# A decoder layer on one core: both branch products of a token half side by side, and the second FFN weight prepared in half-column sets

## The chip, the cores and the metric

The kernel runs on one core of one Trainium2 chip. A core has four compute engines that matter here, each with its own instruction stream that it works through strictly in order: TensorE (PE) multiplies matrices, VectorE (DVE) works element by element on two inputs, ScalarE (ACT) applies functions or copies, GpSimd (POOL) does element-wise work too. SyncE (SP) issues the DMAs, also in order. Engines wait for each other through semaphores. The metric is the device time of the program in microseconds; less is better.

## The reference, cut to what matters

One layer on 1024 tokens of 1024 channels, in float32. Two attention branches A and B (the first 800 us, hardly touched by the change) give `o_a` and `o_b`; then:

```python
merged = (jax.nn.sigmoid(g_a) * (o_a @ w_branch_a[l])
          + jax.nn.sigmoid(g_b) * (o_b @ w_branch_b[l]))
x = _layer_norm(ALPHA * x + merged @ w_out[l], ln1_g[l], ln1_b[l])
gate, up = jnp.split(x @ w_ffn_in[l], 2, axis=-1)
ffn = (jax.nn.silu(gate) * up) @ w_ffn_out[l]
x = _layer_norm(ALPHA * x + ffn, ln2_g[l], ln2_b[l])
```

`w_branch_*` is 512 x 1024, `w_ffn_in` 1024 x 5632, `w_ffn_out` 2816 x 1024.

## The kernel before, in words

**Three products for one.** Every float32 operand of a large product is split into a high part (ACT copies it into a rounded type, `whi`, `w[:, 0]`) and a low part (the rest, by a subtraction on POOL for weights or DVE for activations). `mm3` (lines 95 to 101) then issues three matmuls of 128 x 512 for each term: L99 takes high by high, L100 weight low, L101 activation low. A weight tile is therefore of use only when DMA, ACT and POOL have all been at it.

**Branch stage.** `branch(br, ...)` does all 1024 tokens of branch 0 first: it loads and splits `odr`, and for each of eight column blocks c multiplies both token halves, multiplies by the gate tile `g` (read from `gdr`, four buffers, L549) and writes the result to `mdr` in DRAM. Then the same for branch 1, with `emit_b` reading `mdr` back (`m`, two buffers), adding it and splitting the sum into `MH`, `ML` (L649 to L651). `load_w` loads one tile of `wbr` for two c and both halves (L92 on ACT, L93 on POOL for 1024 columns at once), and a tile of `wout` after every second c.

**Output product and transition.** The `wout` product with its layer norm fills `Y`, then transposes (`turn`, L699 to L701) make the activations of the FFN in the forms that a Strassen-Winograd scheme wants. `c11` of the first `AHEAD` = 2 column blocks (24 matmuls each) is done between the turns.

**FFN1.** A loop over 22 column blocks c. Each has seven products of 12 matmuls: `c11` is two of them, then come s2, s3, s1, s4, a22. Four weight sums r1 to r4 are made on DVE (L818 to L821, tag `ss`, four buffers), each is split by ACT (L770) and POOL (L771), and the products are added up from PSUM (L787 for `c11`, L838 five products in six additions); L846 and L847 are the two gating products m1 and m0. At every odd c one pair j is complete: `wb` (one buffer) gets four quarter blocks of `w_ffn_out` (two loads of 512 KB), which are stored raw three times (L859), combined by four DVE instructions of 128x512 (L860 to L863) and stored four times (L865) into `abd`; the two `h` tiles are treated likewise, stored at L868, combined in place at L869 to L872, stored at L874. So each pair has fourteen 256 KB stores.

**FFN2.** Seven passes p over eleven pairs j; `prepare` loads a 512 KB tile `abd[p][j]` holding both operands and splits it (L898 ACT, L899 DVE, L900 POOL). `closing` adds up the passes and ends in the layer norm; in the last pass the last `LASTC` = 6 tiles are multiplied token tile by token tile so that the norms overlap with products.

**What sets the order.** PE's order is the order in which the code is written (`manual_schedule`). The order on ACT, DVE, POOL and SP is made by a scheduler from priorities and buffer rings when the program is built; at run time every engine keeps to that list.

Of the kernel before, what the change touches and what calls it, by code (L numbers as in the profile page):

```python
# [20 lines left out]
KT = 8  # L21
# [17 lines left out]
AHEAD, LASTC, HURRY = 2, 6, 100  # L39
# [10 lines left out]
def trunk_kernel(ctx: ExitStack, tc: tile.TileContext, xT, xn, wt, wbr, wout, wfi, wfo,  # L50
# [17 lines left out]
    def f(ap):  # L68
        return ap.bitcast(F32)
# [34 lines left out]
    XH = [xm.tile([128, KT, 512], F32R, name=f"xh{h}", tag="x", bufs=4) for h in range(2)]  # L104
    XL = [xm.tile([128, KT, 512], F32R, name=f"xl{h}", tag="x", bufs=4) for h in range(2)]
# [17 lines left out]
    mdr = dram.tile([8, 128, L], F32, name="mdr")  # L123
# [407 lines left out]

    def branch(br, oh, ol, emit):
        for k in range(4):
            raw = bp.tile([128, L], F32, name="oraw", tag="oraw", bufs=2)
            sp.dma_start(raw, odr[br][k])
            act.activation(oh[k], raw, AF.Copy)
            dve.tensor_tensor(ol[k], raw, f(oh[k]), op=OP.subtract)
        for c in range(8):
            if c % 2 == 0:
                wh, wl = load_w(wbr[br, c // 2])  # L540
            b0 = (c % 2) * 512
            for h in range(2):
                s = slice(h * 512, h * 512 + 512)
                g = bp.tile([128, 512], F32, name="g", tag="g", bufs=4)
                sp.dma_start(g, gdr[br][c, :, s])
                ps = ps_b()
                mm3(ps, [(wh[:, b0 + k * 128:b0 + k * 128 + 128], wl[:, b0 + k * 128:b0 + k * 128 + 128],
                          oh[k][:, s], ol[k][:, s]) for k in range(4)])
                dve.scalar_tensor_tensor(g, g, 1.0, ps, op0=OP.add, op1=OP.mult)  # L549
                emit(c, h, g)  # L550
            if c % 2:
                k = br * 4 + c // 2
                load_w(wout[k * 128:k * 128 + 128], WOH[k], WOL[k])

# [84 lines left out]
    OA = [xm.tile([128, 4, L], F32R, name=f"oa{x}", tag="x", bufs=4) for x in range(2)]  # L639
    MH, ML = [], []  # L640
    for h in range(2):
        MH.append(xm.tile([128, KT, 512], F32R, name=f"mh{h}", tag="x", bufs=4))
        ML.append(xm.tile([128, KT, 512], F32R, name=f"ml{h}", tag="x", bufs=4))
    OB = [[bp.tile([128, L], F32R, name=f"ob{x}{k}") for k in range(4)] for x in range(2)]

    def emit_b(c, h, g):
        m = bp.tile([128, 512], F32, name="m", tag="m", bufs=2)
        sp.dma_start(m, mdr[c, :, h * 512:h * 512 + 512])
        dve.tensor_tensor(g, g, m, op=OP.add)  # L649
        act.activation(MH[h][:, c], g, AF.Copy, scale=0.5)  # L650
        dve.scalar_tensor_tensor(ML[h][:, c], g, 0.5, f(MH[h][:, c]), op0=OP.mult, op1=OP.subtract)  # L651

    branch(0, [OA[0][:, k] for k in range(4)], [OA[1][:, k] for k in range(4)],
           lambda c, h, g: sp.dma_start(mdr[c, :, h * 512:h * 512 + 512], g))
    branch(1, OB[0], OB[1], emit_b)
# [6 lines left out]
    fin, _fin = open_pool("fin")  # L662
    Y = [fin.tile([128, D], F32, name=f"y{t}") for t in range(NB)]
    for t in range(NB):
        sp.dma_start(Y[t], xn[t * 128:t * 128 + 128])
# [67 lines left out]
    for t in range(NB):  # L733
        half, c0 = divmod(t * 128, 512)
# [73 lines left out]
    ring[0:0] = [(ffl, f"wt{k}", 1) for k in range(4)]  # L808
    for c in range(FC):
# [7 lines left out]
        r1, r2, r3, r4 = (ffl.tile([128, 512], F32, name="ss", tag="ss", bufs=4) for _ in range(4))  # L817
# [30 lines left out]
        if c % 2 == 0:  # L848
            even = h
            continue  # L850


        j = c // 2
        wb = ffl.tile([128, 2, 1024], F32, name="wb", tag="wb", bufs=1)
        for x in range(2):
            sp.dma_start(wb[:, x], wfo[(c - 1 + x) * 128:(c + x) * 128])
        b11, b12, b21, b22 = wb[:, 0, 0:512], wb[:, 0, 512:1024], wb[:, 1, 0:512], wb[:, 1, 512:1024]
        for p, b in ((1, b11), (2, b21), (3, b22)):
            sp.dma_start(abd[p][j][:, 1], b)  # L859
# [4 lines left out]
        for p, b in ((5, b11), (7, b12), (6, b22), (4, b21)):  # L864
            sp.dma_start(abd[p][j][:, 1], b)  # L865
# [3 lines left out]
        dve.tensor_tensor(a22, a21, a22, op=OP.add)  # L869
        dve.tensor_tensor(a21, a11, a21, op=OP.subtract)  # L870
        dve.tensor_tensor(a11, a22, a11, op=OP.subtract)
        dve.tensor_tensor(a12, a12, a11, op=OP.subtract)  # L872
        for p, a in ((5, a22), (7, a21), (6, a11), (3, a12)):
            sp.dma_start(abd[p][j][:, 0], a)  # L874
# [12 lines left out]
    def prepare(p, j):  # L887
        k = len(fring)
        fring.append(None)
        if k % 2 == 0:  # L890
# [4 lines left out]
        raw = wp.tile([128, 1024], F32, name="wraw", tag="wraw", bufs=2) if k < 7 or k % 3 == 0 else \  # L895
            fe.tile([128, 1024], F32, name="fraw", tag="fraw", bufs=4)
# [21 lines left out]
    def closing(p, t, ps):  # L918
# [5 lines left out]
        elif p == 2:  # L924
            scaled(y[:, ha], ps)
            plus(y[:, ha], u)
            dve.bn_stats(bs[:, 0, :], y[:, ha])
        elif p == 6:
            plus(u, ps)
        elif p == 5:  # L930
            v = fy.tile([128, 512], F32, name="v", tag="v", bufs=2)
            plus(v, ps, u)
# [99 lines left out]
```

## Time and profile before

| | us |
|---|---|
| median of three runs (1681.66 to 1690.01) | 1688.73 |
| the profiled execution | 1686.29 |
| its span | 1684.4 |
| PE busy in it | 1606.5 (95%) |
| DVE, ACT, POOL busy | 1160.9, 771.7, 671.3 |

The profile is one execution. Its page gives busy times of the engines; further views of the same trace list what an engine waited for, the busy time by stretch of the span, groups of instructions by line, the chain of waits, and single instructions in order of time. The stages in this execution: branch products 800 to 911 us, output product 911 to 998, turns and `c11` ahead 998 to 1031, FFN1 1031 to 1457, FFN2 1457 to the end.

### The profile page before, as it was taken

Reading aid. Unit: us, or ns where it says so; the run is one execution under the profiler, and the core shown is the slowest. Engines: PE = TensorE matmul, PEld = TensorE weight load, DVE = VectorE, ACT = ScalarE, POOL = GpSimd, SP = SyncE. Lnnn points to the kernel's source line nnn. Section 1 sums busy time; section 2 is a strip of 40 time slices with the busy share of each in tenths; the row PEclk is TensorE's granted clock in tenths of the full one; section 3 lists DMA queues with packets and bytes.
Section 4 is the critical chain, followed back from the end, with each engine's and each line's share of the span. In section 5 each row is a group of like instructions: output and inputs, shape, how many; then the busy total and the mean of one; then the engine's idle time right before and its main releaser. Section 6 shows DMA issues by size and latency. Waiting matters only on the chain. (4 is left out here: it accounts for less than half of the span.)

```text
span 1684.4 us, 22398 instructions
## 1 busy us (share of the span) xinstructions
PE 1606.5 (95%) x7722; PEld 1312.0 (78%) x7722; DVE 1160.9 (69%) x2016; ACT 771.7 (46%) x1368; POOL 671.3 (40%) x646
## 2 busy tenths in 40 slices
PE   7898999998999999999989998999899999999997
PEld 5776887776888888888767876887778888878885
DVE  6889999979645454544466668868786665557577
ACT  6777878884444444544322024222233323254341
POOL 1122333332333333333432036444455444377673
PEclk9999999999999999999999998999999999999998
DMA  5112212121222222223886115677643332497652
GB/s 176 47 40 65 60 45 59 57 70 43 57 68 61 70 57 74 59 63 124 272 257 242 77 51 175 233 247 257 234 160 120 106 107 93 143 342 272 190 165 93
DMA packets 83817, 216.18 MB, mean 128 GB/s; under 512 B 10164, under 2 KB 14260, under 8 KB 83704
## 3 DMA queue, kind: packets, MB, share of 16 engines
q1 hardware_dynamic: 83704, 214.75, 39.0%
q8 instruction: 61, 1.00, 0.2%
q14 instruction: 52, 0.43, 0.1%
HBM read 139.93 MB, written 65.87 MB: 122 GB/s over the span
## 5 line engine op out<-in xcount | busy, mean ns | idle before, releaser
L99 PE MATMUL mm<-xh,whi 128*128 128x512 f32 (+1 forms) x720 | 296.4, 412 | 15.5 <-ACT whi L146 6.4
L101 PE MATMUL mm<-xl,whi 128*128 128x512 f32 (+1 forms) x720 | 281.9, 392 | 1.2 <-DVE xl L156 1.2
L100 PE MATMUL mm<-xh,wlo 128*128 128x512 f32 (+1 forms) x720 | 281.4, 391 | 0.5 <-DVE wlo L147 0.5
L478 POOL TENSOR_SCALAR p<-p,st 128x512 f32<-128x512 f32 (+1 forms) x192 | 113.3, 598 | 321.3 <-DVE st L475 268.6
L93 POOL TENSOR_TENSOR wlo<-wraw,whi 128x1024 fp32r<-128x1024 f32 x51 | 123.1, 2414 | 192.3 <-ACT whi L92 171.0
L771 POOL TENSOR_TENSOR w<-ss,w 128x512 fp32r<-128x512 f32 x88 | 130.4, 1496 | 165.6 <-ACT w L770 158.2
L101 PEld LDWEIGHTS mm<-xl,whi 128*128 128x128 f32 x720 | 136.1, 189 | 32.2 <-DVE xl L156 2.4
L99 PEld LDWEIGHTS mm<-xh,whi 128*128 128x128 f32 x720 | 136.9, 190 | 29.6 <-issue 6.4
L100 PEld LDWEIGHTS mm<-xh,wlo 128*128 128x128 f32 x720 | 137.3, 191 | 13.0 <-DVE wlo L147 1.0
L503 DVE TENSOR_TENSOR pl<-T,ph 128x512 fp32r<-128x512 f32 (+1 forms) x160 | 100.7, 634 | 36.6 <-ACT ph L502 34.7
L99 PE MATMUL acc<-fs 128*128 128x512 f32 x308 | 120.4, 391 | 2.8 <-ACT fs L898 2.8
L101 PE MATMUL acc<-fs 128*128 128x512 f32 x308 | 120.5, 391 | 0.6 <-POOL fs L900 0.6
L100 PE MATMUL acc<-fs 128*128 128x512 f32 x308 | 120.4, 391 | 0.2 <-DVE fs L899 0.2
L502 ACT ACTIVATE ph<-T 128x512 fp32r<-128x512 f32 (+1 forms) x160 | 87.3, 552 | 38.8 <-PE T L501 34.5
L309 ACT ACTIVATE junk<-sm,nt 128x1024 bf16<-128x1024 f32 (+2 forms) x93 | 96.8, 1040 | 14.6 <-DVE nt L317 12.8
L501 PE MATMUL T<-identf,p 128*128 128x128 f32 x576 | 90.5, 273 | 4.8 <-POOL p L478 2.5
L501 PEld LDWEIGHTS T<-identf,p 128*128 128x128 f32 x576 | 71.2, 140 | 26.8 <-POOL p L478 4.4
L900 POOL TENSOR_TENSOR fs<-fraw,fs 128x512 fp32r<-128x512 f32 x47 | 80.7, 1730 | 27.8 <-ACT fs L898 27.8
L511 PE MATMUL O<-pl,V 128*128 128x256 f32 x320 | 82.8, 282 | 1.8 <-DVE pl L503 1.8
L510 PE MATMUL O<-ph,V 128*128 128x256 f32 x320 | 83.6, 283 | 0.0
L899 DVE TENSOR_TENSOR fs<-fraw,fs 128x512 fp32r<-128x512 f32 x47 | 54.4, 1169 | 39.8 <-ACT fs L898 39.8
L771 POOL TENSOR_TENSOR w<-wraw,w 128x512 fp32r<-128x512 f32 x44 | 64.8, 1485 | 35.7 <-ACT w L770 26.9
(278 smaller groups left out, 4107.5 us busy)
## 6 DMA issues: line engine op xcount, KB each, us to landing
fraw<-abd SPq DMA_DIRECT2D x47, 512.0 KB
wraw<-in_wt_dram SPq DMA_DIRECT2D x45, 512.0 KB
abd<-wb SPq DMA_DIRECT2D x77, 256.0 KB
abd<-h SPq DMA_DIRECT2D x77, 256.0 KB
wraw<-abd SPq DMA_DIRECT2D x30, 512.0 KB
wraw<-in_wfi_dram SPq DMA_DIRECT2D x24, 512.0 KB
wup<-in_wfi_dram SPq DMA_DIRECT2D x22, 512.0 KB
wb<-in_wfo_dram SPq DMA_DIRECT2D x22, 512.0 KB
```

What stands on the lines that cost most here:

```text
L93: pool.tensor_tensor(lo, raw, f(hi), op=OP.subtract)
L99: te.matmul(ps, ah, bh, start=(first and i == 0), stop=False)
L100: te.matmul(ps, al, bh, start=False, stop=False)
L101: te.matmul(ps, ah, bl, start=False, stop=(last and i == n - 1))
L309: act.activation(j[:, :128 * (i + 1)], SM[i], AF.Sign, bias=bias(x), accum_out=s[:, x:x + 1])
L478: pool.tensor_scalar(pc, pc, st[:, 3:4], 1.0, op0=OP.mult, op1=OP.mult)
L501: te.transpose(T[:, s * 128:s * 128 + 128], P[qq][:, j * 128:j * 128 + 128], identf)
L502: act.activation(ph[:, c:], T[:, c:], AF.Copy)
L503: dve.tensor_tensor(pl[:, c:], T[:, c:], f(ph[:, c:]), op=OP.subtract)
L510: te.matmul(O, V[:, j, :], ph[:, r0:r0 + 256], start=(j == 0), stop=False)
L511: te.matmul(O, V[:, j, :], pl[:, r0:r0 + 256], start=False, stop=(last and jj == 1))
L771: pool.tensor_tensor(s[:, 1], raw, f(s[:, 0]), op=OP.subtract)
```

## The change

* Branch stage: the function `branch` is gone. Tokens 512 to 1023 come first; for each token half and each pair of columns, branch 0 and branch 1 are multiplied one behind the other. So every `wbr` tile is loaded and split twice, once for each half. Of its low part POOL makes one half and DVE the other. `mdr` is gone, `g` has seven buffers, `wout` tiles come through a buffer of their own, and tokens are kept in another order afterwards (`TOK`).
* `AHEAD` 2 becomes 3, `LASTC` 6 becomes 10.
* FFN1: the raw quarter blocks are no longer stored into `abd` (FFN2 loads those from `w_ffn_out`). `wb` is loaded and combined for half of the columns at a time, one half set at every c: two loads of 256 KB, four DVE instructions of 128x256, four stores of 128 KB. The combinations q3, q2, q4 of `h` go into the `ss` ring, which has five buffers, instead of in place. Four weight slots move in the ring.
* FFN2: raw tiles 2 to 5 of the first pass use other buffers, the sixth is hurried too, the first four passes load their two halves separately, and the additions of passes 6 and 7 are arranged anew (sixteen DVE instructions in the closing of pass 7 become twelve).

The core of the diff:

```diff
-AHEAD, LASTC, HURRY = 2, 6, 100
+AHEAD, LASTC, HURRY = 3, 10, 100
...
+    for h in (1, 0):
+        s = slice(h * 512, h * 512 + 512)
...
+        load_o(O[0], 0, s)
+        load_o(O[1], 1, s)
+        for c2 in range(4):
+            m = []
+            for br in range(2):
+                raw = load_raw(wbr[br, c2])
+                wh, wl = (wp.tile([128, 1024], F32R, name=n, tag=n, bufs=2) for n in ("whi", "wlo"))
+                act.activation(wh, raw, AF.Copy)
+                pool.tensor_tensor(wl[:, 0:512], raw[:, 0:512], f(wh[:, 0:512]), op=OP.subtract)
+                dve.tensor_tensor(wl[:, 512:1024], raw[:, 512:1024], f(wh[:, 512:1024]), op=OP.subtract)
+                for x in range(2):
+                    c = 2 * c2 + x
+                    g = bp.tile([128, 512], F32, name="g", tag="g", bufs=7)
+                    sp.dma_start(g, gdr[br][c, :, s])
...
+            k = c2 + 4 * (1 - h)
+            raw = load_raw_b(wout[k * 128:k * 128 + 128], [128, 1024])
+            act.activation(WOH[k], raw, AF.Copy)
+            pool.tensor_tensor(WOL[k], raw, f(WOH[k]), op=OP.subtract)
...
-    ring[0:0] = [(ffl, f"wt{k}", 1) for k in range(4)]
+    ring[0:0] = [(ffl, "wt0", 1)]
+    ring += [(ffl, f"wt{k}", 1) for k in range(1, 4)]
...
-        r1, r2, r3, r4 = (ffl.tile([128, 512], F32, name="ss", tag="ss", bufs=4) for _ in range(4))
+        r1, r2, r3, r4 = (ffl.tile([128, 512], F32, name="ss", tag="ss", bufs=5) for _ in range(4))
...
-        if c % 2 == 0:
-            even = h
-            continue
...
-        wb = ffl.tile([128, 2, 1024], F32, name="wb", tag="wb", bufs=1)
-        for x in range(2):
-            sp.dma_start(wb[:, x], wfo[(c - 1 + x) * 128:(c + x) * 128])
-        b11, b12, b21, b22 = wb[:, 0, 0:512], wb[:, 0, 512:1024], wb[:, 1, 0:512], wb[:, 1, 512:1024]
-        for p, b in ((1, b11), (2, b21), (3, b22)):
-            sp.dma_start(abd[p][j][:, 1], b)
+        j, x = divmod(c, 2)
+        cols = slice(x * 256, x * 256 + 256)
+        wb = ffl.tile([128, 4, 256], F32, name="wb", tag="wb", bufs=1)
+        for y in range(2):
+            rows = wfo[(2 * j + y) * 128:(2 * j + y + 1) * 128]
+            sp.dma_start(wb[:, 2 * y:2 * y + 2], rows.rearrange("p (a n) -> p a n", a=2)[:, :, cols])
+        b11, b12, b21, b22 = (wb[:, y] for y in range(4))
...
         for p, b in ((5, b11), (7, b12), (6, b22), (4, b21)):
-            sp.dma_start(abd[p][j][:, 1], b)
+            sp.dma_start(abd[p][j][:, 1, cols], b)
+        if x == 0:
+            even = h
+            continue
...
-        dve.tensor_tensor(a22, a21, a22, op=OP.add)
-        dve.tensor_tensor(a21, a11, a21, op=OP.subtract)
-        dve.tensor_tensor(a11, a22, a11, op=OP.subtract)
-        dve.tensor_tensor(a12, a12, a11, op=OP.subtract)
-        for p, a in ((5, a22), (7, a21), (6, a11), (3, a12)):
+        q2, q3, q4 = (ffl.tile([128, 512], F32, name="ss", tag="ss", bufs=5) for _ in range(3))
+        dve.tensor_tensor(q3, a11, a21, op=OP.subtract)
+        dve.tensor_tensor(a21, a21, a22, op=OP.add)
+        dve.tensor_tensor(q2, a21, a11, op=OP.subtract)
+        dve.tensor_tensor(q4, a12, q2, op=OP.subtract)
+        for p, a in ((7, q3), (5, a21), (6, q2), (3, q4)):
             sp.dma_start(abd[p][j][:, 0], a)
...
+        if 2 <= k < 6:
+            raw = f(wp.tile([128, 1024], F32R, name="w", tag=("whi", "wlo")[k % 2], bufs=2))
+        elif k < 7 or k % 3 == 0:
...
+        if p > 3:
+            sp.dma_start(raw, abd[p][j].rearrange("p a n -> p (a n)"))
+        else:
+            r0, c0 = (2 * j + (p > 1)) * 128, (p > 2) * 512
+            sp.dma_start(raw[:, 512:1024], wfo[r0:r0 + 128, c0:c0 + 512])
+            sp.dma_start(raw[:, 0:512], abd[p][j][:, 0])
```

In the order that the scheduler makes, three places show how instructions move. Lines of the changed kernel are some numbers higher: r1 to r4 are L831 to L834 (L818 to L821 before), the combinations of `wb` L870 to L873 (L860 to L863), the additions from PSUM L851 (L838), `c11`'s L799 (L787), m1 and m0 L859 and L860 (L846 and L847), q3, a21, q2, q4 L884 to L887.

**Place 1, DVE at the end of one column block of FFN1.** Before, at the end of c = 2 (its m0 is L847):

```order
L846 TENSOR_TENSOR h<-h,u 128x512
L838 TENSOR_TENSOR h<-pb,h 128x512
L847 TENSOR_TENSOR h<-h,u 128x512
L818 TENSOR_TENSOR ss<-wup 128x512
L819 TENSOR_TENSOR ss<-ss,wraw 128x512
L787 TENSOR_TENSOR u<-pb,u 128x512
```

The two sums L818 and L819 here are those of c = 5; the sums of c = 3 and c = 4 stand further up. Now, at the end of c = 3 (its m0 is L860):

```order
L886 TENSOR_TENSOR ss<-h 128x512
L860 TENSOR_TENSOR h<-h,u 128x512
L873 TENSOR_TENSOR wb<-wb 128x256
L887 TENSOR_TENSOR ss<-h,ss 128x512
L831 TENSOR_TENSOR ss<-wup 128x512
L832 TENSOR_TENSOR ss<-ss,wraw 128x512
L833 TENSOR_TENSOR ss<-wraw,wup 128x512
L834 TENSOR_TENSOR ss<-wraw,ss 128x512
L799 TENSOR_TENSOR u<-pb,u 128x512
```

The sums that follow here are those of c = 4, the very next block; those of an even c have moved from more than one block ahead to directly behind the last work of the block before it, and c = 5's follow a little later.

**Place 2, DVE at the `wb` combinations of FFN1.** Before, one set in the course of c = 3:

```order
L860 TENSOR_TENSOR wb<-wb 128x512
L820 TENSOR_TENSOR ss<-wraw,wup 128x512
L861 TENSOR_TENSOR wb<-wb 128x512
L838 TENSOR_TENSOR u<-pb,u 128x512
L862 TENSOR_TENSOR wb<-wb 128x512
```

Now, around the step from c = 4 to c = 5, the end of one half set and all but the last row of the next:

```order
L871 TENSOR_TENSOR wb<-wb 128x256
L872 TENSOR_TENSOR wb<-wb 128x256
L873 TENSOR_TENSOR wb<-wb 128x256
L799 TENSOR_TENSOR u<-pb,u 128x512
L851 TENSOR_TENSOR u<-pb,u 128x512
L870 TENSOR_TENSOR wb<-wb 128x256
L871 TENSOR_TENSOR wb<-wb 128x256
L872 TENSOR_TENSOR wb<-wb 128x256
```

Sets of twice the width, about two in a pair of blocks, have become half sets, four in a pair, up to c = 10, all in the same single buffer; here two rows of other work stand between the end of one half set and the start of the next.

**Place 3, POOL at c = 2 of FFN1** (names with numbers, `wup` and `ss` say what is split). Before, in the order in which PE wants them, s2 first and a22 last:

```order
L771 TENSOR_TENSOR w_10325<-ss_10331,w_10325 128x512
L771 TENSOR_TENSOR w_10326<-ss_10332,w_10326 128x512
L771 TENSOR_TENSOR w_10327<-ss_10330,w_10327 128x512
L771 TENSOR_TENSOR w_10328<-ss_10333,w_10328 128x512
L771 TENSOR_TENSOR w_10329<-wup_10321,w_10329 128x512
```

Now s1 (`w_10383`) and a22 (`w_10385`) come ahead of s2 (`w_10381`), behind the two `c11` tiles of c = 3:

```order
L783 TENSOR_TENSOR w_10494<-wraw_10490,w_10494 128x512
L783 TENSOR_TENSOR w_10495<-wraw_10490,w_10495 128x512
L783 TENSOR_TENSOR w_10383<-ss_10386,w_10383 128x512
L783 TENSOR_TENSOR w_10385<-wup_10379,w_10385 128x512
L783 TENSOR_TENSOR w_10381<-ss_10387,w_10381 128x512
```

The split that PE wants first at c = 2 has moved from the first place to the third.

## Rows read from the trace of the kernel before

**Rows 1.** Busy time by stretch (first line names the columns):
```profile
core 0: us, PE busy (x) PEld busy (x) DVE busy (x) ACT busy (x) POOL busy (x), PEclk, DMA share, GB/s
800.00:911.00 111.00, 99.61 (x418) 78.38 (x417) 63.56 (x70) 33.47 (x42) 41.70 (x19) 0.98 0.76 246
...
1036.00:1250.00 214.00, 206.15 (x882) 166.16 (x881) 167.79 (x198) 54.22 (x100) 110.39 (x75) 0.99 0.69 235
1250.00:1457.00 207.00, 207.00 (x898) 168.38 (x898) 129.94 (x163) 64.29 (x105) 103.67 (x74) 1.00 0.31 102
```

**Rows 2.** The same by 5 us, where the granted clock falls:
```profile
1025.00:1030.00 5.00, 1.34 (x2) 0.79 (x3) 4.91 (x5) 2.46 (x5) 3.99 (x3) 0.50 0.14 12
...
1230.00:1235.00 5.00, 3.45 (x9) 2.79 (x10) 4.76 (x9) 0.00 (x0) 0.00 (x0) 0.69 0.62 184
890.00:895.00 5.00, 5.00 (x16) 3.91 (x16) 3.57 (x6) 1.26 (x2) 0.00 (x0) 0.66 0.93 329
...
1480.00:1485.00 5.00, 4.14 (x11) 2.98 (x11) 4.22 (x4) 3.02 (x3) 5.00 (x4) 0.66 0.51 157
```

**Rows 3.** PE's waits, 800 to 911 us (total, times, longest):
```profile
PE ob L99 <- DVE g L549: 5.9, 4, 1.9
PE ob L100 <- POOL wlo L93: 2.7, 2, 1.6
PE ob L99 <- ACT mh L650: 1.3, 1, 1.3
```

**Rows 4.** Groups by line, 801 to 911 us (busy, mean ns | idle before, releasers):
```profile
L549 DVE SCALAR_TENSOR_TENSOR g<-g,ob 128x512 f32<-128x512 f32 x32 | 21.7, 682 | 26.8 <-DMA g<-gdr 23.4 <-PE ob L101 2.8 <-DMA oraw<-odr 0.6
...
L93 POOL TENSOR_TENSOR wlo<-wraw,whi 128x1024 fp32r<-128x1024 f32 x7 | 17.2, 2463 | 27.6 <-ACT whi L92 27.6
```

**Rows 5.** PE's waits, 998 to 1036 us:
```profile
PE pb L99 <- ACT w L770: 5.2, 1, 5.2
PE pb L100 <- POOL w L771: 1.9, 1, 1.9
```

**Rows 6.** PE's waits, 1036 to 1250 us:
```profile
PE pb L99 <- DVE h L838: 3.9, 2, 2.6
PE pb L99 <- DVE u L838: 3.4, 2, 2.7
```

**Rows 7.** DVE groups by line, 1060 to 1245 us:
```profile
L838 DVE TENSOR_TENSOR u<-pb,u 128x512 f32<-128x512 f32 x26 | 17.8, 685 | 0.7
L818 DVE TENSOR_TENSOR ss<-wup 128x512 f32<-128x512 f32 x9 | 13.8, 1533 | 0.0
...
L860 DVE TENSOR_TENSOR wb<-wb 128x512 f32<-128x512 f32 x9 | 10.5, 1162 | 23.4 <-issue 9.7 <-DMA abd<-wb 5.8 <-DMA wraw<-in_wfi_dram 4.8
...
L872 DVE TENSOR_TENSOR h<-h 128x512 f32<-128x512 f32 x5 | 3.4, 687 | 1.0 <-DMA abd<-h 1.0
```

**Rows 8.** Chain of waits, 1060 to 1245 us (start, length, what):
```profile
1124.22 2.00 DMA abd<-wb
1126.29 3.67 DMA wb<-in_wfo_dram
1129.97 4.66 DMA abd<-wb
```

**Rows 9.** ACT and POOL groups by line, 1260 to 1420 us:
```profile
L770 ACT ACTIVATE w<-ss 128x512 fp32r<-128x512 f32 x34 | 21.3, 628 | 26.5 <-PE pb L101 26.5
...
L771 POOL TENSOR_TENSOR w<-ss,w 128x512 fp32r<-128x512 f32 x34 | 49.2, 1448 | 54.5 <-ACT w L770 47.0 <-DVE h L838 7.5
```

**Rows 10.** One line, L526 (duration ns min/median/max):
```profile
L526 DVE TENSOR_TENSOR o<-O,o x64: 396/417/418, 162.3 to 799.7; 64x256 f32<-64x256 f32 x64
```

**Rows 11.** PE's wait for a tile, 1457 to 1490 us:
```profile
PE acc L99 <- ACT fs L898: 2.8, 1, 2.8
```

**Rows 12.** In order of time, the last matmul and the last closing's first instruction:
```profile
1672.72 0.39 PE L101 MATMUL acc<-fs 128*128 128x512 f32 x1
...
1676.02 0.69 DVE L916 TENSOR_TENSOR y<-acc,y 128x512 f32<-128x512 f32 x1
```

## What the change was predicted to do

> **What bounds the kernel now.** Read the busy times by stretch first [rows 1]. Where nothing goes wrong, from 1250 to 1457 us, PE is busy all the time: 898 matmuls in 207 us, one every 0.2305 us. That is the pace to beat; a product of 12 matmuls takes 2.77 us, `c11` 5.53, a column block of FFN1 (84 matmuls) 19.4 and a pair of blocks 38.7. So only places where PE is idle or slowed can give anything, and any new wait of PE costs its whole length. The change adds and removes no matmul. Then read what PE waited for, stage by stage [rows 3, 5, 6, 11], and the granted clock around these waits [rows 2]: behind a wait of some microseconds it falls to between 0.50 and 0.69, which is part of a stretch at 1.2 instead of 2.4 GHz. Last, see which engines are nearly full beside PE: in the first half of FFN1 DVE is busy 167.8 of 214 us, and the chain of waits there runs through the `wb` loads, stores and instructions [rows 1, 8].
>
> **Branch stage.** PE is idle 11.4 of 111 us [rows 1], and 890 to 895 us holds 16 matmuls where 21.7 fit, 1.3 us more [rows 2]: 12.7 in all. The waits are for DVE's L549, 5.9 us, for POOL's low parts, 2.7, and for `mh`, 1.3 [rows 3]. L549 in turn was idle 23.4 us for `g` loads, and one low part takes POOL 2.46 us [rows 4]. The change takes `mdr` away (8 MB written and read), adds 4 MB of `wbr` loads, and gives `g` seven buffers, so that its loads go out early; the stage's DMA traffic falls from 28 to 24 MB at a share of 0.76 now [rows 1]. A `wbr` tile serves 24 matmuls (5.53 us) instead of 48, but POOL makes half of its low part (about 1.3 of the 2.46 us) beside DVE's half of 0.7. I expect left-over waits of 1.2 us at the first gate, and some 2.5 where POOL stands at a `wout` tile (2.43 us of work) ahead of a low part that PE wants: 3.7 in all. Gain 9, between 5 and 12.
>
> **Transition.** PE waits 5.2 us for the first s2 and 1.9 for its low part [rows 5], and runs at a granted clock of 0.50 around it [rows 2]. A third `c11` (5.53 us) is to lie over that. But it takes its own two splits, 2.1 us each on ACT and POOL together [rows 9], and at c = 0 s1 and a22 now stand ahead of s2 on POOL, two splits of 1.45 us. So about 3 us of waiting stay. Gain 4.5, between 2 and 7.
>
> **FFN1, the term that decides.** Now PE waits 7.3 us for L838 [rows 6], and with the lower clock at 1230 us [rows 2] about 9.3 us are lost. The change does three things here.
>
> First, the raw stores go: three of seven 256 KB `wb` stores of a pair. Less DMA work, none of it on PE's path by itself.
>
> Second, the r sums come later (place 1). For an even c everything stands in one chain behind the end of the block before: the last addition 0.69 us [rows 7], q2, m0, q4, r1, r2, then ACT 0.63 and POOL 1.45 [rows 9] until s2 can start. An SBUF instruction takes 0.69 us alone and up to 1.53 beside POOL [rows 7]; over the 14 such groups of that view (111 instructions, the first L818 and the last L872) the mean is 0.97. With 0.7 to 1.0 each the chain is 6.3 to 7.9 us, and `c11` covers 5.53 and 0.23 of the high-part matmul ahead. So 0.5 to 2.1, I take 1.2 us, are lost at every even c without `wb` work (12 to 20): 6 us.
>
> Third, the half sets. All 22 go through one buffer, four in a pair up to c = 10 (place 2). From a set's last instruction to the next set's first lie the landing of a 128 KB store and of two 256 KB loads. The trace has 256 KB stores of 2.00 and 4.66 us and a pair of 512 KB loads of 3.67 [rows 8]; half of the bytes should take between half and all of that. I take 2.35 + 3.0 = 5.35 us, and as bounds 2.0 + 1.8 = 3.8 and 4.6 + 3.7 = 8.3. DVE works in order and stands still in it once the few rows between are done. One round, from r2 of an even c to r2 of the next:
> - r2 to the end of the first set: ACT and POOL 2.1, three products on PE 8.3, then two additions and the rest of the set, 2.9: 13.3 us. The r sums of the odd block fit beside it.
> - turnaround 5.35; second set with q3: 4 x 0.55 + 1.0 = 3.2.
> - turnaround 5.35; third set with one addition: 2.9.
> - turnaround 5.35; fourth set with m1, a21, an addition, q2, m0, q4, r1, r2: 4 x 0.55 + 7 x 1.0 + 0.7 = 9.9.
> Together 29.3 + 16.05 = 45.3 us, where PE wants 38.7: 6.6 us lost a pair. The 0.55 for a 128x256 instruction lies above the 0.42 of a 64x256 one with a PSUM input [rows 10] and half of a full L860, 0.58 [rows 7]. Who waits: everything behind on DVE, so the r sums, ACT and POOL behind them, and PE. Four pairs (c = 4 to 10) make 26 us. In the first pair c = 0 to 2 has its `c11` done ahead, so PE wants only ten products, 27.7 us, while the same round without those rows takes about 41, and POOL does s1 and a22 before s2 (place 3): 13 us, between 8 and 15. The lower clock behind these waits costs perhaps 1 to 1.5 us for each of some such, say 2 in all beyond what the waiting absorbs.
>
> FFN1 after: 13 + 26 + 6 + 2 = 47 instead of 9.3: **a loss of 37**. With the turnaround at 3.8 the round is 40.7 and FFN1 loses 4 x 2 + 8 + 4 = 20, 11 more than now; at 7 it is 50.3 and 4 x 11.6 + 15 + 6 + 2 = 69, 60 more.
>
> A rule speaks against the change here. The trace has 2.00 us for the least of the 256 KB stores [rows 8]. The Trainium skill, "DMA: Bandwidth & Descriptors" (Anatomy of one DMA), gives a DMA about 2.0 us fixed and bytes at 436 GB/s besides, which is an estimate of 2.3 us for 128 KB and 2.6 for 256 KB; the row lies under its 2.6, and no row shows the halves. By that rule a half set waits hardly less than a full one: an estimate of 5.5 us for its turnaround, 45.8 for the round. Another rule would raise the half instructions: the Trainium skill, "SBUF — State Buffer" (Who interferes with whom), says that an instruction with two SBUF inputs and a POOL one that reads SBUF exclude each other for the whole length. L818's 1.53 beside 0.69, and L838 with a PSUM input at a steady 0.685, agree [rows 7]. By that rule halving the width halves the work but not the wait.
>
> **FFN2.** At the start PE waits 2.8 us for a tile [rows 11] and then has 11 matmuls in 4.14 us, where 18 fit [rows 2]: about 5 us. It is the eighth tile, the first one to come through `fraw`, whose load stands on SP behind the `h` stores. Raw tiles 2 to 5 in idle buffers move these loads ahead by several microseconds, and DVE has fewer instructions behind the last product. Gain 5, between 3 and 7. Passes 6 and 7 do their additions elsewhere; DVE has room (the split tile is wanted 8 us after a closing of 12 instructions begins), so nothing.
>
> **Tail.** The last matmul starts at 1672.72 and ends some 0.4 us later, the last closing begins at 1676.02 because DVE is still at the closing before [rows 12]. With ten tiles at the end a token tile's matmuls take 6.8 instead of 4.1 us, more than a closing's 5: it can begin at once. Gain 2.5, between 1.5 and 3.
>
> **Sum.** 9 + 4.5 + 5 + 2.5 = 21 gained, 37 lost: 16 slower. The profiled execution took 1686.3 us, 2.4 under the median: 1702 against the profile, 1704 against the median. Between the single bounds the branch, transition, FFN2 and tail terms give 11.5 to 29.
>
> **Rivals.**
> *A, the `wb` round does not bind* (turnaround near 3.8 us, DVE instructions near 0.7): for it speaks the lighter DMA traffic without the raw stores, against it that today's chain already goes through `wb` and L860 is idle 23.4 us in nine sets [rows 7]. FFN1 then loses 9 even blocks x 1.2 and about 8 at c = 2, 19 in all, 10 more than now: 1689 - 21 + 10 = 1678. **Faster.**
> *B, it binds a little* (turnaround 4.6, round 43; 4.4 x 4 + 11 + 5 = 33, 24 more than now): 1689 - 21 + 24 = 1692. **No change.**
> *C, loads stand behind other transfers on SP* (turnaround 7 us: 3.3, the middle of 2.00 and 4.66, and a full 3.67 [rows 8]): FFN1 loses 60 more, 1689 - 21 + 60 = 1728. **Slower.**
> *D, the branch stage gains nothing*, since twice as many weight tiles and POOL's `wout` work come late; 9 more than the forecast: 1713. **Slower.**
>
> **How the numbers follow.** About 0.5%, 8.4 us, is what a measurement of this kernel can tell from no change. Forecast with C and D on the slower side: 0.58, of it C 0.10 and D 0.08. B 0.22. A 0.20, since the round's length rests on landing times that no row shows for these sizes. The likeliest is 1704. The range leaves out half of A below and most of C above: 1678 to 1727.
>
> **What would show it.** Right: PE waits of 4 to 9 us at s2 of c = 4, 6, 8, 10 and above 8 at c = 2, released by DVE's r2 or POOL behind it; half sets of `wb` some 8 to 11 us apart with DVE idle before L870 for DMA; blocks of c = 2 to 11 near 22.5 us, later ones near 20; in the branch stage less than 5 us of PE idle. Wrong: PE full between 1036 and 1250 us as it is after 1250 now, or `wb` turnarounds under 4 us; then the gains stand alone and the kernel is faster.

## The result and the profile after

The changed kernel takes 1728.25 us (median of six runs, 1724.45 to 1730.66) where the kernel before takes 1687.68 in the same session: a ratio of 1.0242, interval 1.0222 to 1.0263. It is slower, as forecast, but by 40.6 us instead of 16, and 1 us above the upper end of the range. The profiled execution has a span of 1722.7 us, 38.3 more than before. By stage, from first matmuls in the two traces:

| | before | after | difference | forecast |
|---|---|---|---|---|
| start of the branch stage | 801.4 | 801.8 | +0.5 | 0 |
| branch stage and output product, to the first turn | 158.6 | 151.6 | -7.0 | -9 |
| turns and `c11` ahead, at equal work | 66.8 | 60.9 | -5.9 | -4.5 |
| FFN1, at equal work | 430.9 | 482.9 | +52.0 | +37 |
| FFN2 | 215.5 | 217.3 | +1.8 | -5 |
| behind the last matmul | 11.2 | 8.2 | -3.0 | -2.5 |

(Equal work: the third `c11`, 5.53 us, is done in the turns now; the table takes it out there and counts it in FFN1. Before the change the first turn begins at 960.0 us, among the output products, and the first s2 at 1026.8; the table goes by these, not by the 998 and 1031 us of the list of stages.)

Busy times by stretch of the changed kernel; the columns are those of [rows 1]:

```profile
800.00:911.00 111.00, 103.58 (x444) 84.06 (x444) 83.72 (x91) 43.50 (x52) 49.31 (x27) 0.98 0.71 238
...
1036.00:1250.00 214.00, 181.72 (x742) 144.64 (x740) 145.28 (x212) 51.10 (x85) 86.70 (x59) 0.93 0.54 175
1250.00:1457.00 207.00, 195.24 (x822) 156.60 (x823) 127.18 (x154) 60.30 (x99) 102.57 (x70) 0.98 0.30 102
```

Against [rows 1], PE is idle 7.4 instead of 11.4 us in the branch stage. In the first half of FFN1 it is idle 32 us instead of 8, at a granted clock of 0.93; in the second, where it never waited, 12. DVE, which one might suspect to be overloaded, is less busy there than before (145 against 168 us), and the DMA share fell from 0.69 to 0.54. So the engines wait for each other in turn; no engine and no queue is full. What PE waited for, 1036 to 1260 us and 1260 to 1475 us, with the columns of [rows 3]:

```profile
PE pb L99 <- ACT w L782: 26.0, 5, 9.6
PE pb L100 <- POOL w L783: 9.7, 5, 3.7
...
PE pb L100 <- POOL w L783: 10.5, 5, 3.7
```

Before, PE waited for additions from PSUM to free a bank (L838, [rows 6]): DVE was behind with reading results. Now it waits for split weights, high and low part, five times each: at c = 2, 4, 6, 8, 10 for both, at c = 12 to 20 for the low part. These are the s2 of every even c. DVE's own waits, 1036 to 1260 us:

```profile
DVE wb L870 <- DMA wb<-in_wfo_dram: 45.3, 16, 5.1
DVE wb L871 <- DMA wb<-in_wfo_dram: 8.5, 13, 2.3
DVE h L851 <- PE pb L101: 4.1, 3, 1.9
DVE u L851 <- PE pb L101: 3.6, 4, 2.0
```

One round in order of time, from the end of the first half set behind c = 4's sums to c = 6's (start, length, engine, line, operation; idle time before it in brackets):

```profile
1125.88 0.41 DVE L873 TENSOR_TENSOR wb<-wb 128x256 f32<-128x256 f32 x1
...
1131.64 0.43 DVE L870 TENSOR_TENSOR wb<-wb 128x256 f32<-128x256 f32 x1 [2.03 <-DMA wb<-in_wfo_dram]
...
1133.69 0.43 DVE L873 TENSOR_TENSOR wb<-wb 128x256 f32<-128x256 f32 x1
...
1140.72 0.43 DVE L870 TENSOR_TENSOR wb<-wb 128x256 f32<-128x256 f32 x1 [5.12 <-DMA wb<-in_wfo_dram]
...
1142.72 0.41 DVE L873 TENSOR_TENSOR wb<-wb 128x256 f32<-128x256 f32 x1
...
1148.51 0.43 DVE L870 TENSOR_TENSOR wb<-wb 128x256 f32<-128x256 f32 x1 [3.37 <-DMA wb<-in_wfo_dram]
...
1153.08 0.69 DVE L887 TENSOR_TENSOR ss<-h,ss 128x512 f32<-128x512 f32 x1
1153.68 0.69 DVE L831 TENSOR_TENSOR ss<-wup 128x512 f32<-128x512 f32 x1
1154.47 0.69 DVE L832 TENSOR_TENSOR ss<-ss,wraw 128x512 f32<-128x512 f32 x1
```

From the last instruction of a half set to the first of the next are 5.35, 6.6 and 5.4 us; 5.35 was taken. Behind the third of them DVE does 6.6 us of work until r2 of c = 6, and PE stands from 1151.5 to 1155.9:

```profile
1155.88 0.80 PE L99 MATMUL pb<-t2h,w 128*128 128x512 f32 x1 [4.42 <-ACT w L782]
```

The s2 that wait for their high part start at 1061.5, 1109.4, 1155.9, 1203.4 and 1251.5, which gives rounds of 46.5 to 48.1 us, mean 47.5. The s2 of c = 12 starts without a wait at 1294.9 and then stands for its low part until 1299.1. From there on, without `wb` work, the rounds are 40.1 to 41.9, taken from the end of one such wait to the next.

### The profile page after: what moved, and what is told of

It is laid out like the page before. It is cut to its first block, busy times and chain, and to the rows that moved or that the text cites. A ratio compares the mean times of both kernels' runs of the same rounds, so it can differ in the third digit from the quotient of the medians.

```text
span 1722.7 us, 22405 instructions
## 1 busy us (share of the span) xinstructions
PE 1615.2 (94%) x7722; PEld 1317.5 (76%) x7722; DVE 1184.5 (69%) x2076; ACT 787.5 (46%) x1376; POOL 680.9 (40%) x654
## 5 line engine op out<-in xcount | busy, mean ns | idle before, releaser
L783 POOL TENSOR_TENSOR w<-ss,w 128x512 fp32r<-128x512 f32 x88 | 136.2, 1579 | 107.4 <-ACT w L782 107.4
L93 POOL TENSOR_TENSOR wlo<-wraw,whi 128x1024 fp32r<-128x1024 f32 x43 | 103.5, 2406 | 164.3 <-ACT whi L92 143.0
L100 PEld LDWEIGHTS mm<-xh,wlo 128*128 128x128 f32 x720 | 137.4, 191 | 12.9 <-DVE wlo L148 1.0
L783 POOL TENSOR_TENSOR w<-wraw,w 128x512 fp32r<-128x512 f32 x44 | 60.9, 1389 | 92.2 <-ACT w L782 90.5
L782 ACT ACTIVATE w<-ss 128x512 fp32r<-128x512 f32 x88 | 53.6, 629 | 85.4 <-DVE ss L832 26.6
```

What stands on the lines that cost most here:

```text
L93: pool.tensor_tensor(lo, raw, f(hi), op=OP.subtract)
L100: te.matmul(ps, al, bh, start=False, stop=False)
L783: pool.tensor_tensor(s[:, 1], raw, f(s[:, 0]), op=OP.subtract)
```

## The experiments

All are made from the changed kernel, except e6. The times are medians, the ratios against the kernel before on the same chip. FFN1 is its length in the profile, from the first s2 to the last product; it was 431 us before, and 477.5 after (483 at equal work). It comes from one execution each, and the same code scatters in it by some 3 us: e5, with the FFN1 of the changed kernel, has 481.1. The kernel before took 1683.4 to 1687.7 us in the five sessions (the result, e1 to e4, e5 to e8, e9 to e11, e12), so times of different sessions are compared by their ratios.

Two theories were put against each other first. **Theory 1:** the four turnarounds of the one `wb` buffer in a pair make the round. **Theory 2:** the q's, which now stand in the `ss` ring between the r sums, keep the r sums of an even c from being made ahead, and only that puts DVE's stalls in PE's way.

**e1**, the third `c11` taken away again.

```diff
-AHEAD, LASTC, HURRY = 3, 10, 100
+AHEAD, LASTC, HURRY = 2, 10, 100
```

> The changed kernel with two c11 done ahead instead of three (this also frees 4 KB for the next three kernels). If the third c11 is worth what was forecast (4.5 us at the start of FFN1), the median rises from 1728 to about 1732. Rival: c = 2 then has its own c11 (5.53 us) to cover its late s2, where 9.6 and 3.7 us of waiting stand now, so that the one cancels the other: 1726 to 1729, with under 9 us of waiting at c = 2.

1730.2 us (ratio 1.0275, 1.025 to 1.0301), FFN1 483.6. By the ratios it is 5.6 us slower than the changed kernel, with intervals that just overlap. From the first turn to the first s2 this kernel needs 65.3 us, 4.4 more than the changed one at equal work. The waits at c = 2 are 6.2 and 2.9 us instead of 9.6 and 3.7, a `c11` less in front, but FFN1 is no shorter at equal work (483.6 against 483.0), since the waits and slow matmuls behind c = 2 take up the difference. So the first forecast, 4.5 us for the third `c11`, fits better than the rival that c = 2 cancels it.

**e2**, a second `wb` buffer.

```diff
-        wb = ffl.tile([128, 4, 256], F32, name="wb", tag="wb", bufs=1)
+        wb = ffl.tile([128, 4, 256], F32, name="wb", tag="wb", bufs=2)
```

> As e1 with two wb buffers instead of one; the r sums stand where they do now. Theory 1 (the turnaround of the one wb buffer makes the round of 47.5 us): a load has a whole set's time to land, DVE's idle time before L870 (45 us between 1036 and 1260) falls under 10, the rounds up to c = 12 fall to the 40 to 42 us that c = 12 to 20 show, FFN1 gets 25 to 35 us shorter: about 1698. Theory 2 (the late r sums alone hold PE up): the rounds stay above 45 and the time stays at 1720 or more.

1723.56 us (1.0243, 1.0218 to 1.0267), FFN1 474.6: 9 us of the 53. DVE's wait for the loads at L870 fell from 45.6 us in e1 to 10.6 (at L871 it rose from 4.9 to 16.3), and yet PE stood still for 46.9 us instead of 51.3:

```profile
PE pb L99 <- ACT w L782: 26.4, 4, 10.5
PE pb L100 <- POOL w L783: 20.5, 11, 3.7
```

Theory 1 alone is out. Three waits stayed long (c = 2, 4 and 6: 10.5, 4.0 and 6.8 us for the high part), since with two buffers the half sets only moved earlier (the last one ends at 1190 us, in e1 at 1281), and crowd the first three pairs; from c = 8 on the waits are those of the late sums, 1.2 to 3.7 us.

**e3**, the q's in a ring of their own.

```diff
-        q2, q3, q4 = (ffl.tile([128, 512], F32, name="ss", tag="ss", bufs=5) for _ in range(3))
+        q2, q3, q4 = (ffl.tile([128, 512], F32, name="qq", tag="qq", bufs=3) for _ in range(3))
```

(and `ss` back to four buffers)

> As e1 with q2 to q4 in three buffers of their own and four ss buffers for the r sums, as before the change; half sets and the one wb buffer stay. The r sums of a block then stand up to two blocks ahead again. Theory 1 (turnaround): DVE stands still for the loads as long as now, four times a pair, rounds stay above 44 and the time above 1718. Theory 2 (the r sums behind the q's put the four turnarounds in PE's way; the set's own chain, four times 5.7 plus 2.9 = 34 us, is shorter than PE's 38.7): PE's waits between 1036 and 1475 us fall from 46 to under 15, rounds near 39 to 40, the time near 1690.

1693.69 us (1.0051, 1.003 to 1.0073), FFN1 445.9: 38 us of the 53. No wait for a split of an s2 is left behind c = 0; DVE still stands still for `wb` loads, as long as in e1 (45.6):

```profile
DVE wb L870 <- DMA wb<-in_wfo_dram: 44.8, 15, 4.4
```

```profile
PE pb L99 <- DVE h L851: 16.4, 10, 2.7
PE pb L99 <- ACT w L782: 5.3, 1, 5.3
PE pb L99 <- DVE u L851: 1.8, 2, 0.9
PE pb L100 <- POOL w L783: 0.8, 1, 0.8
```

The same 45 us of DVE idle cost PE 51 us in e1 and 24 here (18 of it in FFN1's middle, where under 15 were forecast): whether a stall of DVE matters depends on how far ahead the sums are that stand behind it. The waits that are left are of the kind before the change, [rows 6], only more of them. But theory 2 does not hold alone either. The rounds from c = 0, 2 and 4 are 37.4 to 40.2 us, about as it forecast; those from c = 6, 8 and 10 are 46.5 to 47.2, nearly as long as with late sums; from c = 12 on, without `wb` work, they are 38.7 to 38.9. The rounds from c = 2 and 6, with the columns of [rows 1]:

```profile
1059.20:1098.00 38.80, 38.80 (x170) 31.57 (x169) 25.62 (x40) 10.28 (x20) 18.35 (x14) 1.00 0.58 191
1138.20:1185.40 47.20, 41.29 (x169) 32.40 (x168) 31.14 (x47) 10.62 (x21) 18.89 (x14) 0.96 0.53 173
```

The half sets themselves end when they did, the last one at 1277 us (1281 in e1). Read from these rounds, early sums let PE run ahead of the half sets for three rounds; after that the turnarounds hold PE up again, now through the additions from PSUM. No run tests this by itself.

**e8**, the q's in place as before, with AHEAD 3, LASTC 10 and half sets as changed.

```diff
-        q2, q3, q4 = (ffl.tile([128, 512], F32, name="ss", tag="ss", bufs=5) for _ in range(3))
...
+        dve.tensor_tensor(a22, a21, a22, op=OP.add)
+        dve.tensor_tensor(a21, a11, a21, op=OP.subtract)
+        dve.tensor_tensor(a11, a22, a11, op=OP.subtract)
+        dve.tensor_tensor(a12, a12, a11, op=OP.subtract)
```

> The changed kernel (AHEAD 3, LASTC 10, half sets in one buffer) with only the combinations of h in place again and four ss buffers. Theory 2 (the q's in the ss ring put the r sums late): as in e3, rounds fall from 47.5 to 40 or 41, no wait over 4 us at an s2, and the time is 1728 - 36 = about 1692. If e3 gained by its three further buffers rather than by the order, less than half of that comes back: over 1710.

1697.62 us (1.0077, 1.0061 to 1.0093), FFN1 446.1, 31 less than the changed kernel's 477.5, with one buffer fewer. So most of e3's gain comes without added room; what makes the other 7 us is not shown. By the ratios the time is 28 us less than the changed kernel's, where 36 were forecast, and the rounds are not 40 or 41 throughout: those from c = 4 to 10 are 44.1 to 48.3 us, the later ones 38.7 to 38.9.

**e4**, full sets again, one per pair, the q's in the ring.

```diff
-        cols = slice(x * 256, x * 256 + 256)
-        wb = ffl.tile([128, 4, 256], F32, name="wb", tag="wb", bufs=1)
+        cols = slice(0, 512)
+        wb = ffl.tile([128, 2, 1024], F32, name="wb", tag="wb", bufs=1)
+        for x in range(2):
+            sp.dma_start(wb[:, x], wfo[(c - 1 + x) * 128:(c + x) * 128])
```

> As e1 with full sets again (two loads of 512 KB, four instructions of 128x512 and four stores of 256 KB at every odd c, still no raw stores), the q's still in the ss ring. Half as many turnarounds, each longer (about 2.4 + 4.2 = 6.6 us): if turnarounds are what counts, two of 6.6 instead of four of 5.7 save some 9 us a pair, rounds near 41 and a time near 1702; if it is the late r sums, rounds stay near 47 and the time near 1728.

1708.51 us (1.0146, 1.0127 to 1.0166), FFN1 463.8: 20 us less than e1, the rounds up to c = 12 43.1 to 46.3. The time lies between the two figures, because both theories hold a part: the half sets cost 20 us (e1 to e4), the late sums 38 (e1 to e3), and taking both away, 62 (e1 to e7 below), is about their sum, though e7 also has the weight slots in the order of before.

**e9**, q's in place, half sets in two buffers, AHEAD 2, LASTC 6.

```diff
-        wb = ffl.tile([128, 4, 256], F32, name="wb", tag="wb", bufs=1)
+        wb = ffl.tile([128, 4, 256], F32, name="wb", tag="wb", bufs=2)
```

> As e7 (q's in place, four ss buffers, AHEAD 2, LASTC 6, no raw stores) but with half sets of wb in two buffers, and the new order of weight slots. If half sets cost only by their single buffer, FFN1 is as long as in e7 (422 us) and the time 1675. If twice as many instructions and DMAs cost by themselves (DVE and POOL share SBUF, the rest of the loss of e3 and e8), FFN1 is 430 us or more and the time 1683 or more.

1687.74 us (1.0004, 0.9993 to 1.0014), FFN1 442.5, 21 more than e7. So FFN1 with half sets stays long even with early sums and a second buffer. By the ratios only 10 us of it are left at the end: FFN2 is 6 us shorter than in e7, without the wait at its start that e7 has.

**e12**, full sets as in e7, but every combination in two instructions of 128x256.

```diff
+        for y in (slice(0, 256), slice(256, 512)):
+            dve.tensor_tensor(b11[:, y], b12[:, y], b11[:, y], op=OP.subtract)
...
```

> As e7 (full wb sets, loads and stores of full width, one buffer), but each of the four combining instructions is issued as two of 128x256. It tells apart why the half sets of e9 cost FFN1 21 us against e7. If the instructions do it (a half one beside POOL takes 1.5 us like a full one, 0.42 alone: 88 of them took 60.6 us in e9, 44 full ones 45.7 in e7), FFN1 is 8 to 20 us longer than the 421.6 of e7 and the time 1683 to 1695. If the doubled loads, stores and waits did it, FFN1 stays within 3 us of e7 and the time is 1675 to 1678.

1679.87 us (0.9966, 0.9952 to 0.998), FFN1 429.5, 7.8 more than e7, and a time between the two forecasts. So a good third of e9's 21 us goes with the doubled number of instructions; by the ratios it is 3.5 us, with intervals that overlap. That the other 13 us are the doubled loads, stores and waits for them follows only by subtraction, since e9 also has the changed order of weight slots.

**e7**, in FFN1 only the raw stores are left out; full sets, q's in place, AHEAD 2, LASTC 6, the branch stage and FFN2 loads as changed (the edit is that of e4 and e8 together, with the ring of weight slots as before).

> New branch stage and new FFN2 start, and in FFN1 of the change only what leaves work out (no raw stores); full wb sets, q's in place, four ss buffers, the order of weight slots, AHEAD 2 and LASTC 6 as before. If the late r sums and the turnarounds are the whole loss of FFN1, it is at most 431 us long again, and the branch stage (7 us) and FFN2's start (6 us) remain: 13 us less than before, ratio 0.992. If something else of the change costs, as the loads of w_ffn_out in FFN2, the ratio is 0.998 or more.

1674.9 us (0.9945, 0.9927 to 0.9964): 9 us less than before, between the two forecasts. FFN1 is 421.6 us long, 9 less than before: between 1036 and 1443 us PE waits 0.5 us in all.

```profile
PE pb L99 <- DVE u L850: 0.3, 1, 0.3
PE pb L99 <- DVE h L850: 0.2, 1, 0.2
```

So dropping the raw stores is worth what [rows 6] and the clock behind those waits had cost; the rest of FFN1's change cost 62 us (e1 against e7). But FFN2 starts with a wait of 4.0 us:

```profile
PE acc L99 <- ACT fs L918: 4.0, 1, 4.0
```

**e6**, the kernel before with the new branch stage alone (its edit is the first half of the diff of the change).

> The kernel before with the new branch stage alone (two token halves, both branches side by side, split low parts, no mdr); FFN1, FFN2, AHEAD 2 and LASTC 6 as before. The branch stage was 7 us shorter in the changed kernel (9 forecast): 7 us less than before, a ratio near 0.996. If the gain was given back in the transition, where the first s2 waits for its load and its sums in any case, the ratio is 1.000.

1680.48 us (0.9969, 0.9957 to 0.9981), 4.5 less by medians and 5.2 by the ratio, interval 3.2 to 7.2. The gain of this part holds, a little under the 7 us.

**e5**, LASTC alone.

```diff
-AHEAD, LASTC, HURRY = 3, 10, 100
+AHEAD, LASTC, HURRY = 3, 6, 100
```

> The changed kernel with LASTC 6 instead of 10, nothing else. The wait of 5.9 us on DVE's L923 at the end of FFN2 and the lower clock behind it should go (6 to 8 us), because the last tile is wanted 11 us later; the end behind the last matmul should grow from 8.2 to about 11.2 us, as before the change. Net 3 to 5 us less: about 1724. If the tile is late for another reason (its load), the wait stays and the time is about 1731.

1723.89 us (1.0237, 1.0221 to 1.0254). FFN2 is 209.6 us instead of 217.3 and has no wait of PE in it; behind the last matmul it is 11.1 us instead of 8.2. These two stages give the 3 to 5 us that were forecast, and the median is 4.4 below the changed kernel's; but by the ratios, each against the kernel before in its session, it is only 0.8 us and no difference.

**e10**, e7 with the last pair's q's in the idle `wb` buffer, and LASTC 7.

```diff
+        if j == PAIRS - 1:
+            qt = ffl.tile([128, 2, 1024], F32, name="wb", tag="wb", bufs=1)
+            q2, q3, q4 = qt[:, 0, 0:512], qt[:, 0, 512:1024], qt[:, 1, 0:512]
```

> As e7, with the q's of the last pair alone in a buffer of their own (the wb one, which is idle by then) and LASTC 7. In the changed kernel the start of FFN2 had no wait, in e7 one of 4 us stands at the eighth tile, whose load stands behind the last in-place q's and their stores on SP. If that order is the reason, the wait goes with its lower clock: 5 to 6 us less than e7, and 1 to 2 more from the tail: about 1668. If the load is late by the traffic alone, 1674.

1671.26 us (0.9899, 0.9877 to 0.9922), 8 us less than e7 by the ratios, as forecast. The wait at the start of FFN2 falls from 4.0 to 0.9 us. So raw tiles 2 to 5, which e7 has too, do not take this wait away by themselves. That the place of the q's did it in the changed kernel does not follow: e8 and e9 have the q's in place and no such wait, but the changed order of weight slots; e12, with the order of before, waits 4.6 us. What that order moves was not traced.

**e11**, e10 with AHEAD 3 and three instead of four weight slots.

```diff
-    ring[0:0] = [(ffl, "wt0", 1)]
-    ring += [(ffl, f"wt{k}", 1) for k in range(1, 4)]
+    ring[0:0] = [(ffl, f"wt{k}", 1) for k in range(3)]
```

> As e10 with AHEAD 3 and three weight slots of that ring instead of four (the third u tile takes their room). The third c11 covers the wait of 5.2 us for the first s2: 4 to 5 us less than e10, about 1664, if the missing slot costs nothing; if splits then wait for slots, PE waits inside FFN1 and the time is 1668 or more.

**1662.01 us (ratio 0.9857, 0.9841 to 0.9873)**: faster than both kernels, by 24 and 66 us. From 1015 us to the end of FFN1 PE's waits are down to two kinds:

```profile
PE pb L99 <- DVE h L850: 3.1, 2, 2.4
PE pb L100 <- POOL w L783: 2.5, 1, 2.5
```

and the first half of FFN1 reads, against [rows 1]:

```profile
1036.00:1250.00 214.00, 210.86 (x910) 170.23 (x909) 175.37 (x213) 59.72 (x109) 116.21 (x78) 1.00 0.59 202
```

DVE is busier there than in the kernels before and after (168 and 145 us), and PE hardly waits.

## Why the prediction was right in its direction and short in its size

**Right: the deciding term and its place.** FFN1 turned from a small loss into the largest one; the waits stand at the s2 of every even c, as placed, through the chain that was written down. Turnarounds of 5.35, 6.6 and 5.4 us against 5.35 taken. Counted from start to start of the matmuls, against 0.2305 us, the waits lost 14.0 us at c = 2 against 13, and 25.0 at c = 4 to 10 against 26. The second agreement is partly luck. The round is 47.5 us and not 45.3, and its parts differ both ways. In the round from c = 6 to 8 it takes 17.4 us from r2 of c = 6 to the end of the first set, where 13.3 were taken: "The r sums of the odd block fit beside it" failed, since r3 and r4 of c = 6 and the four of c = 7, four of these six at 1.6 to 1.8 us beside POOL, fill most of DVE's time until 1164.2. The other three sets with the work between took 12.9 instead of 16.0, the turnarounds 17.2 instead of 16.05. With the 14.0 and 11.5 us of the next two paragraphs FFN1 lost 64.5 us by this count, where the sum had 47. Of the signs named beforehand one failed: PE is idle 7.4 us in the branch stage, not under 5.

**The first mis-sized term: the clock, 2 us forecast, 14 measured.** Adding up in FFN1 the matmuls that start more than 0.3 us behind the one before without a wait between, 70 of them lost 14.0 us against the usual 0.2305 (24 and 4.2 us before the change): 1.5 us at c = 0, 1.6 to 2.5 at each of c = 2 to 12, 0.1 to 0.2 behind each of the short waits after. What the sum left out is that each of the long waits is followed by such a stretch. Behind the wait that ends at 1061.5 us:

```profile
1058.00:1063.00 5.00, 0.79 (x1) 0.28 (x1) 3.91 (x8) 2.77 (x5) 2.49 (x1) 0.50 0.59 210
1063.00:1068.00 5.00, 2.01 (x5) 1.63 (x6) 4.92 (x4) 0.70 (x2) 5.00 (x5) 0.50 0.56 143
1068.00:1073.00 5.00, 5.00 (x19) 3.92 (x18) 3.88 (x3) 1.83 (x3) 5.00 (x4) 0.76 0.39 123
1073.00:1078.00 5.00, 5.00 (x23) 4.11 (x22) 2.36 (x4) 1.27 (x2) 4.08 (x4) 1.00 0.69 213
```

0.50 is the level of 1.2 GHz; the matmuls follow each other at 0.43 us up to the one at 1069.99 and at 0.23 from the one at 1070.40 on. [rows 2] had shown just this behind three waits of the kernel before, and the loss there, 1 to 2 us each, was written down; applied to the five long waits that were forecast it would have given 5 to 10 instead of "2 in all". "What the waiting absorbs" was an argument without a row. The runs do not refute it: between the s2 of c = 4 and of c = 10 DVE waited for PE only 3 us in all, so full speed there might have left PE waiting longer. By rounds instead, a pair lost 8.8 us where 6.6 were forecast.

**The second: c = 12 to 20, 6 us forecast, 11.5 measured.** The chain of late sums was taken at 1.2 us of loss for each, with one split on POOL. The waits are 3.7, 1.2, 2.2, 1.2 and 2.2 us, all for the low part (11.5 counted from start to start), while r1 and r2 of these blocks take 0.69 us each, as taken. What the term left out is POOL's order, place 3: the split of s2 is POOL's first at c = 14 and 18, its second at c = 16 and 20, and at c = 12 its third, behind s1 and a22. The prediction had counted this at c = 0 and 2 only. At c = 12, where s2's split is the first of the three in the last row:

```profile
1293.92 1.79 POOL L783 TENSOR_TENSOR w<-ss,w 128x512 fp32r<-128x512 f32 x1 [5.22 <-ACT w L782]
1295.68 1.71 POOL L783 TENSOR_TENSOR w<-wup,w 128x512 fp32r<-128x512 f32 x1
1297.35 4.63 POOL L783 TENSOR_TENSOR w<-ss,w 128x512 fp32r<-128x512 f32 x3
```

**The third: FFN2, 5 us gained by the forecast, 1.8 lost.** The start did gain: it has no wait, though not by raw tiles 2 to 5 alone, as was forecast (e7 has them and waits 4.0 us). But a new one came at the end of FFN2, in a place that the prediction had looked at and valued at nothing:

```profile
PE acc L100 <- DVE fs L923: 5.9, 1, 5.9
```

"The split tile is wanted 8 us after a closing of 12 instructions begins" compared the closing's 7.2 us with a start right at the end of pass 7. In the trace the closing starts later, at 1683.9 us, because DVE first waits for the three tiles ahead, whose loads were issued from 1673.4 on; it ends at 1691.1, and PE has been out of tiles since 1686.0. The step that failed is to start a chain from the engine's own work without asking when that engine would be free. With LASTC 6 the tile is wanted later, and e5 shows both sides: 7.7 us back in FFN2, 2.9 us lost behind it.

**Smaller ones.** The branch stage gained 7.0 instead of 9 in the profile (5.2 by e6), with POOL's low parts as the last wait, as expected, but for 5.7 us and not 2.5:

```profile
PE ob L100 <- POOL wlo L646: 5.7, 3, 2.7
```

The turns gained 5.9 instead of 4.5; e1, without the third `c11`, loses 4.4 of it again. The tail gained 3.0 instead of 2.5.

**The cause, which the prediction had half.** It described one chain and gave nearly all of the loss to the turnarounds (39 us, and 6 to the late sums). Four kernels with two `c11` ahead and one `wb` buffer set the two against each other. FFN1 is 483.6 us with late sums and half sets (e1), 445.9 with early sums (e3), 463.8 with full sets (e4), 421.6 with both (e7, which also has the weight slots in the order of before). So the late sums cost 38 to 42 us, the half sets 20 to 24. From the first s2 to that of c = 12, when the `wb` work is over, both count: 278.1, 257.4, 259.8 and 232.9 us, which is 21 to 27 for the late sums and 18 to 25 for the half sets. Behind it the late sums cost 15 to 17 and the half sets under 2. With a second buffer and the sums late, 9 us go (e2). Of the half sets' cost up to 8 us go with the doubled instructions (e12). Rival C, the longer turnaround, met the measured time by its number and not by its mechanism: from c = 4 on the turnarounds that end with a wait for loads are 5.2 to 6.6 us, not 7; the fourth of each pair is 11.6 to 11.7, filled with r sums. Not settled is how much of the rest of the half sets' cost is the smaller loads and how much the order of the weight slots.

Halving the sets did not halve the waits: the turnarounds with full sets in e4 begin at 5.6 us, and five of its ten lie under 6.7. The estimate of 5.5 us for half sets came from the Trainium skill, "DMA: Bandwidth & Descriptors" (Anatomy of one DMA); its fit is for transfers that GpSimd issues, while these go out from SP, so that the trace comes near it is no test of it. In e9 half an instruction takes 0.42 us alone and up to 1.5 beside a POOL split. The Trainium skill, "SBUF — State Buffer" (Who interferes with whom), says that a DVE instruction with two SBUF inputs contends with a GpSimd one that reads SBUF, and the rows of the last section agree with it.

## What to carry to other kernels

A buffer ring is an order: a tile that is added to a ring between two others makes the later one wait for its last reader, and here three tiles with a DMA store behind them took away the lead that hid a part of DVE's stalls. When an engine stalls as long as before and its neighbour waits anew, ask what stood ahead of the stall, before making the stall shorter. Look up in each engine's order where the piece stands that is wanted first, for every block and not only for the first ones. And count the slow matmuls behind a long wait with every such wait, from the rows that show them, rather than once for all.

## What was not expected of the hardware

An element-wise instruction of half the width is not half as dear when two engines work beside each other. Full combinations in e7 and half ones in e9 (groups by line, 1022 to 1230 us):

```profile
L871 DVE TENSOR_TENSOR wb<-wb 128x512 f32<-128x512 f32 x11 | 11.3, 1029 | 16.2 <-DMA wb<-in_wfo_dram 16.1
```

```profile
L870 DVE TENSOR_TENSOR wb<-wb 128x256 f32<-128x256 f32 x22 | 15.4, 702 | 19.1 <-DMA wb<-in_wfo_dram 15.2 <-DMA abd<-wb 2.6 <-issue 1.2
```

Both are the first of the four combinations. In e9 in order of time, three POOL splits and half instructions beside and behind them:

```profile
1115.60 4.16 POOL L783 TENSOR_TENSOR w<-ss,w 128x512 fp32r<-128x512 f32 x3 [9.14 <-ACT w L782]
...
1117.10 1.51 DVE L870 TENSOR_TENSOR wb<-wb 128x256 f32<-128x256 f32 x1
1118.52 1.51 DVE L872 TENSOR_TENSOR wb<-wb 128x256 f32<-128x256 f32 x1
...
1120.56 0.41 DVE L873 TENSOR_TENSOR wb<-wb 128x256 f32<-128x256 f32 x1
```

Eleven full sets take DVE 45.7 us in all, the same work in 22 half sets 60.6: the sum of the four lines of each kernel. Alone, a full instruction takes 0.69 us in e7 and a half one 0.42 in e9; beside POOL they go up to 1.8 and 1.5.
